# Layer parameters loaded and turned ahead of the modulation's products, rotary tables behind the normed rows, in a two-layer trunk

## The chip, the core and the metric

The kernel runs on one core of a Trainium2 chip. The metric is device time in microseconds (us), the median of several executions. The engines are named as in the profile: PE is the matrix engine (PEld its weight loads), DVE, ACT and POOL are the three elementwise engines, SP issues most of the DMAs, and a trailing q ("SPq", "ACTq", "POOLq") marks an engine's instruction queue, where DMAs are issued.

## What is computed

A trunk of two layers over 1024 rows of width 1024, cut here to what matters at the start:

```
c_act = silu(c)
for l in range(2):
    mod = c_act @ ada_w[l] + ada_b[l]                  # 1024 x 6144
    sh1, sc1, gt1, sh2, sc2, gt2 = split(mod, 6)
    h = rms_norm(x, norm1_g[l]) * (1.0 + sc1) + sh1
    proj = h @ w_in[l]                                 # q, k, v and the RWKV inputs
    q, k = partial_rotary(q, cos, sin), partial_rotary(k, cos, sin)
    mixed = concat(diff_attention(q, k, v), rwkv7_time_mix(proj[..., 1536:])) @ w_out[l]
    x = x + gt1 * mixed
    h2 = rms_norm(x, norm2_g[l]) * (1.0 + sc2) + sh2
    x = x + gt2 * hier_moe(h2)                         # 32 experts, two for each row
return rms_norm(x, final_g)
```

`cos` and `sin` come from the positions alone.

## The kernel before

Each engine works through its own instruction list in order. The kernel is traced in Python, and then a scheduler with a model of the engines' times lays out the order of each list; `issue_after(x)` adds no wait of its own but forbids the scheduler to put the instructions of its block ahead of `x` in the list of `x`'s engine. So both the text of the program and the model decide what stands ahead of what.

The start of layer 0 goes like this. `before()` in `build` makes constants, loads the first four of the eight tiles of x (128 rows each), and runs `modulation(0, range(4), ...)`: blocks 0 to 3, which give the shift `sh1` and the scale `sc1`. A block is four loads of `ada_w` (512 KB each, called chunks below), 32 narrow products into `ada_ps` (L238, eight for each chunk), an addition of the bias on DVE into `modE` (L241), a turn of `modE` on PE into `ada_t` (L244), and a copy into the table `mv` on DVE (L245). Then, behind the last `ada_w` load, `params(0, ...)` fetches 14 small rows through POOL's queue into `prow`, turns them on PE (`prow_ps`, L276) and copies them into `pv` on DVE (L279); `first_weights` fetches and splits the first two slices of `w_in` (`wa_raw` into `wa_hi` and `wa_lo`, L348 and L349); and the last four tiles of x are loaded.

`norm1` takes the squares of a tile on ACT (L317, into `n_j`), the inverse root for two tiles at a time (L100 on DVE, L102 on ACT, L107 to L109 on DVE, ending in `rs_y_n`), scales the rows (`n_y`, L325), turns them on PE (`n_t`, L332), and applies scale `g1` (L328, from `mv` and `pv`) and shift on ACT (`n_tmp`, L334). DVE and ACT split the result into `hh` and `hl` (L337, L338), and PE multiplies both with `wa_hi` and `wa_lo` into `pj` (L361 to L363). `prow_ps` and `n_t` share two PSUM banks. The eight 128-column pieces of a half of the rows are gone through one by one, and the second half follows.

From there on `phase_a` weaves projections, the RWKV scan (tiles `rb_*`, with the state `b_sb`) and attention (`at_*`). Between them PE does what `more` yields: the modulation's blocks 4 to 11 of layer 0 and all 12 of layer 1 in chunks with two buffers, and after the first eight chunks `tables`, which makes the rotary tables (`rotary_tables`, L159 to L199) and loads layer 1's parameters. Then come the output projection and the mixture of experts, and layer 1 does the same again.

Of the kernel before, what the change touches and what calls it, by code (L numbers as in the profile page):

```python
# [10 lines left out]
F32 = mybir.dt.float32  # L11
# [4 lines left out]
OP = mybir.AluOpType  # L16
# [36 lines left out]
class Trunk:  # L53
# [243 lines left out]
    def norm1(self, l, tile_of, work, psum):  # L297

        nc = self.nc
        self.hh = [self.big.tile([128, T], F32R, name=f"hh{k}", tag=f"hh{k}") for k in range(NK)]  # L300
        self.hl = [self.big.tile([128, T], F32R, name=f"hl{k}", tag=f"hl{k}") for k in range(NK)]
        g1 = work.tile([128, 8], F32, name="g1")
        xs, order = [], ExitStack()
        for g in range(2):
            if g and l:

                for x in (root, xs[-1][1]):
                    order.enter_context(self.tc.issue_after(x.ins))
            if g:
                xs = []  # L310
            for i in range(4):
                if i % 2 == 0:
                    ss = work.tile([128, 2], F32, name="n1_ss", tag="n1_ss", bufs=2)
                    pair = []
                x = tile_of(4 * g + i)
                junk = work.tile([128, D], F32, name="n1_j", tag="n1_j", bufs=1)
                nc.scalar.activation(junk, x, AF.Square, accum_out=ss[:, i % 2:i % 2 + 1])  # L317
                pair.append(x)
                if i % 2:
                    rs = self.rsqrt(work, ss, 2, NORM_EPS, 1.0 / D, "n1", act=True)  # L320
                    root = self.last_root
                    for q, x in enumerate(pair):
                        y = work.tile([128, D], F32, name="n1_y", tag="n1_y", bufs=4)
                        xs.append((y, nc.scalar.activation(y, x, AF.Copy, scale=rs[:, q:q + 1]) if l else
                                   nc.vector.tensor_scalar(y, x, rs[:, q:q + 1], None, op0=OP.mult)))  # L325
            order.close()
            if g == 0:
                nc.vector.scalar_tensor_tensor(g1, self.mv[l][:, 8:16], 1.0, self.pv[l][0][:, 0:8], op0=OP.add, op1=OP.mult)  # L328
            for k in range(NK):
                pt = psum.tile([128, 4, 128], F32, name="n1_t", tag="aa")  # L330
                for i in range(4):
                    nc.tensor.transpose(pt[:, i, :], xs[i][0][:, k * 128:(k + 1) * 128], self.ident)  # L332
                tmp = work.tile([128, 512], F32, name="n1_tmp", tag="n1_tmp", bufs=2)
                nc.scalar.activation(tmp, pt.rearrange("p a b -> p (a b)"), AF.Identity,  # L334
                                     bias=self.mv[l][:, k:k + 1], scale=g1[:, k:k + 1])
                hi, lo = self.hh[k][:, 512 * g:512 * g + 512], self.hl[k][:, 512 * g:512 * g + 512]
                (nc.scalar.copy if k % 2 else nc.vector.tensor_copy)(hi, tmp)  # L337
                nc.vector.tensor_tensor(lo, tmp, hi.bitcast(F32), op=OP.subtract)  # L338


    def split_w(self, wp, l, i, eng=None):
# [79 lines left out]
    def phase_a(self, l, x_src, psum, here, there):  # L421

        nc, a, tc = self.nc, self.a, self.tc
# [10 lines left out]
        more = iter(())  # L434
        if l == 0:
            wpool = sm.enter_context(self.pool(name="adaw", bufs=2, side=there))
            work = sm.enter_context(self.pool(name="adax", bufs=1, side=there))
            rows = self.modulation(0, range(4, 12), wpool, work, psum, 2)
            more = itertools.chain(itertools.islice(rows, 8), self.tables(work, psum), rows,
                                   *(self.modulation(j, range(12), wpool, work, psum, 2) for j in range(1, L)))  # L440

        def wtile(c0):
# [171 lines left out]
        if True:  # L614
            self.when["R", 0] = 0.0
            self.agents = []
            for rank, g in ((0, self.rwkv_second(l, late, sf, there, psum)), (4, firsts()), (6, projects()), (7, tables()), (8, tail()),
                            (9, heads())):
                self.add(rank, g)
            self.weave()  # L620
# [1202 lines left out]
    def final(self, pool):  # L1823
# [4 lines left out]
        for t in range(0, NT, 2):  # L1828
# [7 lines left out]
            for i in range(2):  # L1836
                nc.vector.scalar_tensor_tensor(os[i], self.xm[:, t + i, :], rs[:, i:i + 1], fg, op0=OP.mult, op1=OP.mult)  # L1837
                nc.scalar.dma_start(self.out[0, 128 * (t + i):128 * (t + i) + 128, :], os[i])  # L1838

    def tables(self, work, psum):  # L1840

        self.clear_tinv(work)
        yield
        self.rotary_tables(work)
        yield
        for l in range(1, L):
            self.params(l, work, psum)
            yield
# [73 lines left out]
    def build(self):  # L1922
        ctx, nc = self.ctx, self.nc
        self.cst = ctx.enter_context(self.pool(name="cst", bufs=1))
        self.lay = ctx.enter_context(self.pool(name="lay", bufs=1))
        self.dram = ctx.enter_context(self.pool(name="dram", bufs=1, space=DRAM))
        self.mrow, self.mv, self.pv, xs = {}, {}, {}, []

        def before():
            work = self.norm_pool  # L1930
            self.constants()
            self.conditioning(work, self.psum)

            def load(t):
                x = work.tile([128, D], F32, name=f"x{t}")
                nc.sync.dma_start(x, self.a["x"][0, 128 * t:128 * t + 128, :])
                xs.append(x)

            for t in range(4):
                load(t)  # L1940
            with ExitStack() as s:
                wpool = s.enter_context(self.pool(name="ada0", bufs=13))
                for _ in self.modulation(0, range(4), wpool, work, self.psum, 2):
                    pass
            with self.tc.issue_after(self.ada_load.ins):
                self.params(0, work, self.psum)
                self.first_weights(0)
                for t in range(4, 8):
                    load(t)

        self.start(0, "left", lambda t: xs[t], before)
        x_src = lambda t: self.a["x"][0, 128 * t:128 * t + 128, :]
        for l in range(self.layers):
            x_src = self.layer(l, x_src)
# [48 lines left out]
```

## Time and profile before

| What | Value |
|---|---|
| Median of 3 runs | 2689.37 us (2685.37 to 2702.67) |
| The profiled execution | 2696.09 us, span of its instructions 2694.1 us |
| PE busy | 2389.1 us, 89% of the span |
| DVE busy | 1852.7 us, 69% |
| ACT busy | 1193.2 us, 44% |
| POOL busy | 313.7 us, 12% |
| Mean granted clock of PE | 0.918 |

The profile is one execution. Its shares are averages over stages with different limits: the change touches the first 100 us, where PE is idle for a good part, so the stretch's own rows count there and not the 89%. A granted clock of 1.00 in a row is 2.4 GHz, 0.50 is 1.2 GHz, and values between are means over a stretch that has both.

### The profile page before, as it was taken

The page shows a single profiled execution, that of the slowest core. Times are in us where ns is not written, and L with a number is a line of the kernel's source. Part 1 is how long each engine was busy: PE and PEld are TensorE (multiplying, and loading weights), DVE is VectorE, ACT ScalarE, POOL GpSimd, SP SyncE. Part 2 cuts the span into 40 slices and gives each one's busy share as a digit, 9 for nine tenths or more (in the row PEclk, how much of TensorE's full clock was granted, in tenths as well). Part 3 has the DMA queues.
Part 4 walks back from the last instruction along what each step waited for, and adds up shares of the span by engine and source line. Part 5 has one row for each costly group of instructions (what it writes and reads, how often), then busy time and mean ns, then how long its engine had stood idle before and what let it go on. Part 6 is the DMA issues. An engine that isn't in the chain of part 4 may idle for free. (4 is left out here: it accounts for less than half of the span.)

```text
span 2694.1 us, 45448 instructions
## 1 busy us (share of the span) xinstructions
PE 2389.1 (89%) x17313; PEld 1826.6 (68%) x17313; DVE 1852.7 (69%) x4053; ACT 1193.2 (44%) x2316; POOL 313.7 (12%) x251
## 2 busy tenths in 40 slices
PE   6999998898889979999959989989997996999992
PEld 3666666777767866777736767767776885677771
DVE  4347767656579486877764588965658847787775
ACT  3344443234256224555545555424426622555552
POOL 3100000000000002333310000000000001333330
PEclk8998998789989979999979989899988997999996
DMA  8566765525354247999942434445336325899985
GB/s 295 175 214 205 211 210 166 155 91 148 93 171 126 95 171 290 354 338 359 369 174 103 147 113 143 141 140 166 117 89 193 104 97 195 319 385 348 336 307 202
DMA packets 263940, 542.68 MB, mean 201 GB/s; under 512 B 76504, under 2 KB 180896, under 8 KB 234784
## 3 DMA queue, kind: packets, MB, share of 16 engines
q1 hardware_dynamic: 235712, 484.61, 53.9%
q0 software_dynamic: 23376, 40.99, 4.1%
q10 hardware_dynamic: 4624, 14.06, 1.4%
q8 instruction: 141, 2.31, 0.4%
q14 instruction: 87, 0.71, 0.1%
HBM read 459.29 MB, written 120.09 MB: 215 GB/s over the span
## 5 line engine op out<-in xcount | busy, mean ns | idle before, releaser
L1646 DVE TENSOR_TENSOR w_lo<-w_gu,w_hi 128x2048 fp32r<-128x2048 f32 x134 | 306.3, 2286 | 69.2 <-ACT w_hi L1645 69.0
L1645 ACT CAST w_hi<-w_gu 128x2048 fp32r<-128x2048 f32 x134 | 255.7, 1908 | 211.2 <-PE h_ps L1698 204.5
L361 PE MATMUL pj<-hh,wa_hi 128*128 128x512 f32 x800 | 335.2, 419 | 2.1 <-ACT wa_hi L348 1.7
L362 PE MATMUL pj<-hl,wa_hi 128*128 128x512 f32 x800 | 332.2, 415 | 1.1 <-DVE hl L338 1.0
L363 PE MATMUL pj<-hh,wa_lo 128*128 128x512 f32 x800 | 325.5, 408 | 0.1
L1737 PE MATMUL y_ps<-w_d,hT 128*128 128x512 f32 x560 | 252.2, 593 | 3.4 <-ACTq L1798 2.4
L1697 PE MATMUL h_ps<-w_hi,xT_hi 128*128 128x512 f32 x560 | 243.0, 434 | 4.4 <-ACT xT_hi L1681 4.4
L1698 PE MATMUL h_ps<-w_hi,xT_lo 128*128 128x512 f32 x560 | 222.6, 398 | 2.5 <-DVE xT_lo L1682 2.5
L1699 PE MATMUL h_ps<-w_lo,xT_hi 128*128 128x512 f32 x560 | 222.4, 397 | 0.0
L1726 POOL DMA_INDIRECT yd<-yo,idx_s x70 | 183.6, 2623 | 290.2 <-DVE yo L1723 275.4
L361 PEld LDWEIGHTS pj<-hh,wa_hi 128*128 128x128 f32 x800 | 156.2, 195 | 41.5 <-issue 6.0
L362 PEld LDWEIGHTS pj<-hl,wa_hi 128*128 128x128 f32 x800 | 155.8, 195 | 37.0 <-issue 4.0
L363 PEld LDWEIGHTS pj<-hh,wa_lo 128*128 128x128 f32 x800 | 155.2, 194 | 35.4 <-issue 3.6
L1737 PEld LDWEIGHTS y_ps<-w_d,hT 128*128 128x128 f32 x560 | 100.9, 190 | 104.8 <-issue 100.4
L1697 PEld LDWEIGHTS h_ps<-w_hi,xT_hi 128*128 128x128 f32 x560 | 107.3, 192 | 38.0 <-issue 11.5
L1698 PEld LDWEIGHTS h_ps<-w_hi,xT_lo 128*128 128x128 f32 x560 | 107.3, 192 | 36.7 <-DVE th L1689 11.5
L1682 DVE TENSOR_TENSOR xT_lo<-xT_ps,xT_hi 128x1024 fp32r<-128x1024 f32 x70 | 85.7, 1225 | 65.8 <-ACT xT_hi L1681 65.8
L1699 PEld LDWEIGHTS h_ps<-w_lo,xT_hi 128*128 128x128 f32 x560 | 107.0, 191 | 23.0
L1723 DVE SCALAR_TENSOR_TENSOR yo<-y_ps,wsl,gt 128x1024 f32<-128x1024 f32 x70 | 89.8, 1283 | 38.3 <-PE y_ps L1737 38.3
L1192 ACT ACTIVATE at_p<-at_s,at_mx 128x256 f32<-128x256 f32 (+7 forms) x128 | 94.8, 741 | 40.6 <-DVE at_mx L1190 39.8
L1190 DVE TENSOR_REDUCE at_mx<-at_s 128x1 f32<-128x256 f32 (+7 forms) x128 | 95.6, 752 | 14.5 <-PE at_s L1188 13.3
L238 PE MATMUL ada_ps<-ada_w,crep 128*32 128x128 f32 x1536 | 71.9, 313 | 37.6 <-DMA ada_w<-in_ada_w 37.4
(436 smaller groups left out, 4949.3 us busy)
## 6 DMA issues: line engine op xcount, KB each, us to landing
w_gu<-in_moe_w_gu SPq DMA_DIRECT2D x140, 1024.0 KB
w_d<-in_moe_w_down SPq DMA_DIRECT2D x70, 1024.0 KB
ada_w<-in_ada_w SPq DMA_DIRECT2D x96, 512.0 KB
wa_raw<-in_w_in SPq DMA_DIRECT2D x50, 512.0 KB
sp_z<-z SPq DMA_DIRECT2D x32, 768.0 KB
b_zz<-sp_z SPq DMA_DIRECT2D x32, 512.0 KB
cy<-yd SPq DMA_DIRECT2D x16, 1024.0 KB
qkv<-qst SPq DMA_DIRECT2D x48, 256.0 KB
```

What stands on the lines that cost most here:

```text
L361: nc.tensor.matmul(ps, hi[:, k, :], self.hh[k][:, sl], start=(k == 0), stop=False)
L362: nc.tensor.matmul(ps, hi[:, k, :], self.hl[k][:, sl], start=False, stop=False)
L363: nc.tensor.matmul(ps, lo[:, k, :], self.hh[k][:, sl], start=False, stop=(k == NK - 1))
L1190: nc.vector.tensor_reduce(mx, ps[:, 0:n], axis=AX.X, op=OP.max, negate=True)
L1192: nc.scalar.activation(pm[:, 0:n], ps[:, 0:n], AF.Exp, bias=mx, accum_out=hs["s"][:, t, m:m + 1])
L1645: self.nc.scalar.copy(hi, raw)
L1646: eng.tensor_tensor(lo, raw, hi.bitcast(F32), op=OP.subtract)
L1697: nc.tensor.matmul(ph, hi[:, k, :], whi[:, k % 4, :], start=(k == 0), stop=False)
L1698: nc.tensor.matmul(ph, lo[:, k, :], whi[:, k % 4, :], start=False, stop=False)
L1699: nc.tensor.matmul(ph, hi[:, k, :], wlo[:, k % 4, :], start=False, stop=(k == NK - 1))
L1726: st = nc.gpsimd.indirect_dma_start(out=self.yd, out_offset=bass.IndirectOffsetOnAxis(ap=self.idx_s[:, e:e + 1], axis=0), in_=yos[e % 2], ...
L1737: nc.tensor.matmul(po[:, 512 * half:512 * half + 512], hT[:, k, :], w[:, k, 512 * half:512 * half + 512], start=(k == 0), stop=(k == 1))
```

## The change

`params(0, ...)` is called ahead of the modulation's blocks 0 to 3, outside the block that stands behind the last `ada_w` load. And each step of `tables` is traced inside `issue_after(self.last_lo)`: no instruction of the rotary tables and of layer 1's parameters may stand ahead of the last `hl` of `norm1` in DVE's list.

```
@@ norm1
-                nc.vector.tensor_tensor(lo, tmp, hi.bitcast(F32), op=OP.subtract)
+                self.last_lo = nc.vector.tensor_tensor(lo, tmp, hi.bitcast(F32), op=OP.subtract)
@@ phase_a
-            more = itertools.chain(itertools.islice(rows, 8), self.tables(work, psum), rows,
+            more = itertools.chain(itertools.islice(rows, 8), self.behind(self.last_lo, self.tables(work, psum)), rows,
@@ new
+    def behind(self, x, g):
+
+        while True:
+            with self.tc.issue_after(x.ins):
+                try:
+                    next(g)
+                except StopIteration:
+                    return
+            yield
@@ build, before()
+            self.params(0, work, self.psum)
             with ExitStack() as s:
                 wpool = s.enter_context(self.pool(name="ada0", bufs=13))
                 for _ in self.modulation(0, range(4), wpool, work, self.psum, 2):
                     pass
             with self.tc.issue_after(self.ada_load.ins):
-                self.params(0, work, self.psum)
                 self.first_weights(0)
```

The scheduler lays the lists out anew. Three places follow. In DVE's list, after the scaled rows of the first four tiles of x, there stood before (`modE` is a block's sum with its bias, `mv` its copy, `rs_*_500` the inverse root for x's fifth and sixth tiles):

```order
L325 TENSOR_SCALAR n_y<-x_131,rs_y_n_411 128x1024
L241 TENSOR_TENSOR modE<-ada_ps,ada_bias 128x128
L245 COPY mv_122<-ada_t 128x4
L241 TENSOR_TENSOR modE<-ada_ps,ada_bias 128x128
L245 COPY mv_122<-ada_t 128x4
L241 TENSOR_TENSOR modE<-ada_ps,ada_bias 128x128
L245 COPY mv_122<-ada_t 128x4
L241 TENSOR_TENSOR modE<-ada_ps,ada_bias 128x128
L165 MEMSET freq 128x1
L348 CAST wa_hi<-wa_raw 128x1024
```

and now, in the same list from the split of the first slice of `w_in` on (the five operations of `params` stand between `n_y` and this):

```order
L348 CAST wa_hi<-wa_raw 128x1024
L349 TENSOR_TENSOR wa_lo<-wa_raw,wa_hi 128x1024
L100 TENSOR_SCALAR rs_v_n_500<-n_ss 128x2
L107 SCALAR_TENSOR_TENSOR rs_u_n_502<-rs_v_n_500,rs_y_n_501 128x2
L108 TENSOR_TENSOR rs_u_n_502<-rs_u_n_502,rs_y_n_501 128x2
L109 SCALAR_TENSOR_TENSOR rs_y_n_501<-rs_u_n_502,rs_y_n_501 128x2
L241 TENSOR_TENSOR modE<-ada_ps,ada_bias 128x128
L100 TENSOR_SCALAR rs_v_n_517<-n_ss 128x2
L245 COPY mv_122<-ada_t 128x4
```

The first `modE`, block 0's, has moved behind the split of the first slice and behind the root of the fifth and sixth tiles; the other three blocks' follow later still.

In PE's list, from its first instructions on, before:

```order
L207 MATMUL c_ps<-ident,crow 128x8
L238 MATMUL ada_ps<-ada_w,crep 32x128 x32
L244 MATMUL ada_t<-ident,modE 128x128
L238 MATMUL ada_ps<-ada_w,crep 32x128 x32
L244 MATMUL ada_t<-ident,modE 128x128
L238 MATMUL ada_ps<-ada_w,crep 32x128 x32
L244 MATMUL ada_t<-ident,modE 128x128
L238 MATMUL ada_ps<-ada_w,crep 32x128 x32
L244 MATMUL ada_t<-ident,modE 128x128
L276 MATMUL prow_ps<-ident,prow 128x42
L332 MATMUL n_t<-ident,n_y 128x128 x8
L238 MATMUL ada_ps<-ada_w,crep 32x128 x8
```

and now:

```order
L238 MATMUL ada_ps<-ada_w,crep 32x128 x32
L276 MATMUL prow_ps<-ident,prow 128x42
L332 MATMUL n_t<-ident,n_y 128x128 x8
L244 MATMUL ada_t<-ident,modE 128x128
L238 MATMUL ada_ps<-ada_w,crep 32x128 x32
L244 MATMUL ada_t<-ident,modE 128x128
L238 MATMUL ada_ps<-ada_w,crep 32x128 x32
L244 MATMUL ada_t<-ident,modE 128x128
L238 MATMUL ada_ps<-ada_w,crep 32x128 x32
L244 MATMUL ada_t<-ident,modE 128x128
L238 MATMUL ada_ps<-ada_w,crep 32x128 x8
L332 MATMUL n_t<-ident,n_y 128x128 x4
```

The turn of the parameters and the first eight turns of normed rows have moved ahead of block 0's turn; the products of blocks 1 to 3 still stand behind that turn, and block 4's first chunk directly behind block 3's turn.

In SP's list of DMAs, after the last tile of x, before:

```order
L235 DMA ada_w<-in_ada_w 128x1024 x2
L160 DMA pos_i<-in_positions 128x8x1
L345 DMA wa_raw<-in_w_in 128x1024
L877 DMA b_lnx<-in_rwkv_lnx_g 128x128
L877 DMA b_lnx<-in_rwkv_lnx_b 128x128
L235 DMA ada_w<-in_ada_w 128x1024 x2
L345 DMA wa_raw<-in_w_in 128x1024
```

and now:

```order
L345 DMA wa_raw<-in_w_in 128x1024 x2
L235 DMA ada_w<-in_ada_w 128x1024 x2
L160 DMA pos_i<-in_positions 128x8x1
L877 DMA b_lnx<-in_rwkv_lnx_g 128x128
L877 DMA b_lnx<-in_rwkv_lnx_b 128x128
L235 DMA ada_w<-in_ada_w 128x1024 x10
```

The second and third slice of `w_in` have moved ahead of block 4's first two chunks. Those chunks still take memory that block 3's last products free.

## Rows read from the trace of the kernel before

**Rows 1.** The page: busy time, share of the span and instructions of each engine.

```profile
PE 2389.1 (89%) x17313; PEld 1826.6 (68%) x17313; DVE 1852.7 (69%) x4053; ACT 1193.2 (44%) x2316; POOL 313.7 (12%) x251
```

**Rows 2.** Stretches: length, busy time by engine, granted PE clock, DMA share, GB/s.

```profile
28.00:30.00 2.00, 1.08 (x16) 0.59 (x16) 0.00 (x0) 0.00 (x0) 1.65 (x4) 0.50 1.03 390
...
44.50:50.00 5.50, 5.46 (x44) 3.99 (x45) 4.87 (x17) 4.18 (x7) 0.00 (x0) 0.50 0.58 174
...
50.00:55.00 5.00, 5.00 (x53) 3.59 (x51) 4.24 (x11) 3.15 (x5) 0.00 (x0) 0.98 0.79 216
...
80.00:90.00 10.00, 10.00 (x76) 5.13 (x65) 3.21 (x6) 4.65 (x6) 0.00 (x0) 1.00 0.35 116
```

**Rows 3.** One stretch, from the first to the tenth chunk of blocks 4 to 6.

```profile
44.54:72.55 28.01, 25.19 (x239) 17.65 (x239) 20.70 (x55) 17.51 (x27) 0.00 (x0) 0.90 0.64 198
```

**Rows 4.** PE in order of time: start, length, what, count, idle before and releaser.

```profile
19.18 3.02 PE L238 MATMUL ada_ps<-ada_w,crep 128*32 128x128 f32 x48
...
31.91 4.19 PE L238 MATMUL ada_ps<-ada_w,crep 128*32 128x128 f32 x64
...
41.88 1.12 PE L332 MATMUL n_t<-ident,n_y 128*128 128x128 f32 x4 [3.54 <-DVE pv L279]
44.54 1.08 PE L238 MATMUL ada_ps<-ada_w,crep 128*32 128x128 f32 x16 [1.55 <-DMA ada_w<-in_ada_w]
```

**Rows 5.** DVE in order of time.

```profile
31.16 0.29 DVE L241 TENSOR_TENSOR modE<-ada_ps,ada_bias 128x128 f32<-128x128 f32 x1 [6.96 <-PE ada_ps L238]
...
36.17 0.29 DVE L241 TENSOR_TENSOR modE<-ada_ps,ada_bias 128x128 f32<-128x128 f32 x1 [3.99 <-PE ada_ps L238]
...
37.11 0.16 DVE L245 COPY mv<-ada_t 128x4 f32<-128x4 f32 x1
...
41.55 0.16 DVE L109 SCALAR_TENSOR_TENSOR rs_y_n<-rs_u_n,rs_y_n 128x2 f32<-128x2 f32 x1
41.62 0.20 DVE L279 COPY pv<-prow_ps 128x42 f32<-128x42 f32 x1
...
42.15 0.16 DVE L328 SCALAR_TENSOR_TENSOR g<-mv,pv 128x8 f32<-128x8 f32 x1
```

**Rows 6.** ACT in order of time: squares of the sixth and eighth tile, first scaled piece.

```profile
39.53 1.06 ACT L317 ACTIVATE n_j<-x 128x1024 f32<-128x1024 f32 x1 [0.80 <-DMA x<-in_x]
...
43.31 1.06 ACT L317 ACTIVATE n_j<-x 128x1024 f32<-128x1024 f32 x1 [0.99 <-DMA x<-in_x]
...
44.36 0.76 ACT L334 ACTIVATE n_tmp<-n_t,mv,g 128x512 f32<-128x512 f32 x1
```

**Rows 7.** SP's DMA issues in order of time.

```profile
25.85 5.56 SPq L1936 DMA_DIRECT2D x<-in_x  x4
36.17 1.57 SPq L235 DMA_DIRECT2D ada_w<-in_ada_w  x2
...
53.34 20.98 SPq L235 DMA_DIRECT2D ada_w<-in_ada_w  x8
```

**Rows 8.** PE's chunks of blocks 4 to 6, in order of time.

```profile
47.88 1.08 PE L238 MATMUL ada_ps<-ada_w,crep 128*32 128x128 f32 x16
...
58.15 0.64 PE L238 MATMUL ada_ps<-ada_w,crep 128*32 128x128 f32 x16 [0.52 <-DMA ada_w<-in_ada_w]
60.56 0.64 PE L238 MATMUL ada_ps<-ada_w,crep 128*32 128x128 f32 x16 [0.48 <-DMA ada_w<-in_ada_w]
...
72.55 0.64 PE L238 MATMUL ada_ps<-ada_w,crep 128*32 128x128 f32 x14
```

**Rows 9.** DVE's groups of 47 to 66 us by shape; the table's first use.

```profile
L185 DVE TENSOR_TENSOR ang_r<-ang_r,ang_m 128x64 f32<-128x64 f32 x2 | 0.4, 221 | 0.0
...
L1054 DVE TENSOR_TENSOR xc<-qst,cos x32: 273/282/289, 341.7 to 2006.6; 128x128 f32<-128x128 f32 x32
```

**Rows 10.** What PE waited for, 300 to 850 us; a stretch in it.

```profile
PE rb_s L896 <- DVE b_sb L898: 15.7, 11, 4.2
...
450.00:500.00 50.00, 39.78 (x411) 31.97 (x406) 41.11 (x120) 13.03 (x30) 0.00 (x0) 0.67 0.53 132
```

## The prediction, made before the changed kernel ran

> **What bounds the kernel now.** Read the page first: PE is busy for 89% of the span [rows 1], so a delay of PE early on has little room to be made up for later. The change touches the first 100 us, so next come the stretches there, the waits of PE, and then each engine in order of time. Up to about 44 us the start lives on loads: the DMA share is 1.03 with PE at work for 1.08 of 2.00 us [rows 2], and the last four tiles of x, issued from 25.85 on [rows 7], reach ACT as late as 39.53 (sixth) and 43.31 (eighth) [rows 6]. In this time PE computes blocks 0 to 3 as their chunks come: block 1 starts at 19.18, block 3 runs from 31.91 and ends at 36.1 [rows 4], and the last copy into `mv` ends at 37.3 [rows 5]. Two things then stand in a row behind x's sixth tile: DVE's list has the root of tiles five and six (ends 41.71) ahead of `pv` (41.62) and `g1` (42.15) [rows 5], and PE, which needs the PSUM bank of `prow_ps`, stands for 3.54 us [rows 4]. The first `n_tmp` starts at 44.36, on the heels of the eighth tile's square [rows 6]. From 44.5 to about 75 us PE, ACT, DVE and the chunks of blocks 4 to 6 keep each other waiting; from 80 us PE is the bound, 10.00 of 10.00 us [rows 2].
>
> **The change, part 1: the parameters early.** The 14 loads and the turn of `prow` now end long before they are needed, and the 3.54 us wait for `pv` goes. That alone buys almost nothing: behind that wait the next thing late is ACT, whose list still holds the squares of all four late tiles ahead of the first `n_tmp`, and that one followed the eighth square directly [rows 6]. `ada_bias` is now queued on POOL behind these 14 loads. Its first reader is block 0's `modE`, which will be late for another reason, so I cost this at nothing; without that cover it would be some microseconds.
>
> **Part 2: what the new order does to DVE and PE.** This is where I see the price. Block 0's `modE` now stands in DVE's list behind the split of the first `w_in` slice and behind the root of x's fifth and sixth tiles. In the trace that root ends at 41.71 [rows 5]. PE's list has block 0's turn, which needs this `modE`, ahead of the products of blocks 1 to 3. So PE, which now begins block 1 at 19.18, will stand from about 20 us until about 41, with all 12 chunks lying ready (13 buffers).
>
> Step by step. The sixth tile may land a little earlier, because two chunks (1 MB) issued at 36.17 [rows 7] are no longer in its way, while a `w_in` slice of half that size is instead. I bound the root's end by 39.7 (two microseconds for the whole MB) and 41.7 (no change) and take the middle, 40.7. From a `modE` to the next block's first product the trace has 31.16 to 31.91, or 0.75 us [rows 4, 5]: block 1 starts at 41.45. A block's products take 4.19 us at the low clock [rows 4] and 4 x 0.64 = 2.56 us at the full one [rows 8]; between blocks lie 0.85 us (the 0.75, and a tenth for the end of the products before). All three at the low clock end at 41.45 + 3 x 4.2 + 2 x 0.85 = 55.75; with only the first at it, at 52.5. PE will come out of 20 idle microseconds; in the trace it was at 0.50 (1.2 GHz) in sparse work from 28 us on, worked densely from 44.5, and was at 0.98 in the stretch from 50 [rows 2], so after some 5.5 us. The same span here gives the full clock at about 47, early in block 2, and an end at **52.8**. In the trace that end was 36.1.
>
> From the last `modE` to the end of its `mv` copy it is 1.1 us [rows 5], and `g1` takes 0.2 more: the first `n_tmp` starts at 54.3, where it started at 44.36. So the roots of the last tiles are no longer the bound, and `pv` never was.
>
> **Part 3: the first chunk of block 4.** PE's list has it right behind block 3's turn, and its load takes memory that block 3's last products free: in the trace it was issued at 36.17 [rows 7], 0.07 after those ended, and its products waited till 44.54 [rows 4]. Now the issue comes at 52.9. With the queue less full, an issue took 4.8 us to its products (53.34 to 58.15, the wait for the DMA shown) [rows 7, 8]; the nearest lower bound is 2.4 us, at which chunks follow each other (58.15, 60.56) [rows 8]. I take 4.8, since this one is a whole load behind its issue: 57.7, against 44.54, so **+13.2 us**. Behind it on PE stand the next turns of rows, and all of `norm1` behind those.
>
> The Trainium skill ("DMA: Bandwidth & Descriptors", its table of the two cost components) gives about 2.0 us fixed and the bytes at 436 GB/s, 3.2 us for 512 KB by an estimate from it. The 4.8 us measured here are longer, with other loads in flight; by the page the step would be 1.6 us smaller.
>
> **Part 4: what the norm stage gives back.** From the first chunk of block 4 to the tenth it took 44.54 to 72.55, 28.0 us [rows 3]. In it 5.5 us went by at the low clock [rows 2], and DVE worked out the rotary tables: 20 operations of some 0.22 us [rows 9], 4.4 us. Both go out of the stage. What remains are two buffers: a chunk that is freed comes back after 4.8 us, and its products take 0.64 [rows 8], so two chunks for 5.44 us. The second chunk's products started 3.3 us behind the first's (47.88) [rows 8]; four rounds more make 25.1 us. So -2.9 us. The ends are 0 (the turns and `n_tmp` set the pace as before) and -5.5 (all of the 2.8 us in which PE idles there, 28.01 less 25.19 [rows 3], and half of 5.46 us at the low clock [rows 2]).
>
> **Part 5: the tables late.** These operations and eight small fills now stand behind the last `hl`, at 85 to 105 us, where DVE is busy 3.21 of 10 us [rows 2], and the tables' first reader comes at 341.7 [rows 9]. PE hides them: nothing. If they pushed a `pj` bank's emptying they would cost PE at most their 4.4 us once. Layer 1's parameters go with them and have even more room.
>
> **Part 6: the rest.** PE's list is the same from about 76 to 440 us, and PE-bound, so the delay is carried on. Behind that the lists of both layers' scan and attention stretches are reordered in places, with the same work: of the 32 scan steps one has another number of projections ahead of it, and six another number of attention products, by 3 to 7. I take zero, with some 10 us either way.
>
> **Sum.** +13.2 - 2.9 = +10.3 us. The profiled execution took 2696.1 (its span 2694.1), 6.7 over the median; it would become 2706.4, and the median 2689.4 + 10.3 = **2699.7**. By the bounds: early tile, short load and full give-back, 10.3 - 1 - 2.4 - 2.6 = +4.3; late tile, low clock throughout, no give-back, 10.3 + 1 + 3 + 2.9 = +17.2. The likeliest case's own range is 2693 to 2707.
>
> **Rivals.**
> 1. *Not slower: the reordered scan stretches fill PE's waits.* Between 300 and 850 us PE waits 11 times, 15.7 us, for the scan's state `b_sb` on DVE [rows 10]. The new order moves attention products past some scan steps exactly there. Filling all of it gives 2699.7 - 15.7 = 2684. It decides from two thirds of these waits on. Against it: the scan steps have kept their places against the projections. 0.12.
> 2. *Slower by over 1%: the clock.* In 450 to 500 us the granted clock is 0.67 with PE busy 39.78 us [rows 10]; if a reordered wait sends another such stretch to 0.50, its 40 us cost 20 more: 2720. It decides from about 17 us on. 0.07.
> 3. *The change does what its words say.* If block 0's `modE` is not held up, `pv` is early, the tables' 4.4 us leave DVE in a stretch where it is busy 4.87 of 5.5 us [rows 2], and up to 4 us come of it: 2685.5. It needs the root of the sixth tile done before about 19 us, and that tile is issued after 25.85 [rows 7], or a DVE that takes its list out of order. 0.03.
>
> **How the numbers follow.** The forecast has 0.75; another 0.03 is for what I don't see. 1% of the time before, 27 us, is about what a measurement here can tell from no change. The forecast and rivals 1 and 3 lie within it; over 27 us slower come from rival 2 and the far end of part 6: 0.08. Faster by that much would take more than every wait of rival 1: 0.02. Within: 0.90. The range covers rival 1's 2684 and stops short of rival 2: 2683 to 2717.
>
> **What would show it.** Right: PE idle from about 20 to 41 us behind L244 with DVE's `modE` as releaser; the first `modE` at about 40.7; blocks 1 to 3 in one run, the first of them at 1.08 us a chunk; the first `n_tmp` at 54; block 4's first chunk near 57.7 after a wait for its DMA, and the tenth about 25 us on; no wait for `pv`. PE's rows of 100 us should come 10 us later, and the start of the experts in layer 0 too. Wrong: a first `modE` near 18 (rival 3), or a delay at 100 us that is gone by 850 (rival 1).

## The result, and the profile after

The changed kernel took **2710.27 us** (median of 16 runs) beside 2693.44 us of the kernel before (16 runs on the same chip): a ratio of **1.0055, 95% interval 1.0039 to 1.0070**, some 15 us slower and well within 1%. A second timing (experiment 8) gave 1.0049 (1.0030 to 1.0068). One execution each of experiments 4 and 11, at 8233 and 5558 us, is left out of the ratios below. The profiled execution took 2716.71 us, 6.4 above its own median, and its mean granted clock, 0.913, is the lowest of the 16 (their median is 0.9215), so its later offsets are read with care.

The page: PE is busy for 3 us more than before, in a span that is 20.8 longer, so most of what was lost is standing [rows 1].

```profile
PE 2392.3 (88%) x17313; PEld 1832.6 (68%) x17313; DVE 1857.8 (68%) x4053; ACT 1193.7 (44%) x2316; POOL 314.8 (12%) x251
```

PE in order of time answers to [rows 4]. Block 0's turn (L244) starts after 21.40 us of standing for DVE's `modE`; then blocks 1 to 3 go through in one run, 64 products a row; then the first chunk of block 4 stands for its load.

```profile
39.58 0.48 PE L244 MATMUL ada_t<-ident,modE 128*128 128x128 f32 x1 [21.40 <-DVE modE L241]
39.98 3.45 PE L238 MATMUL ada_ps<-ada_w,crep 128*32 128x128 f32 x64
...
44.12 1.95 PE L238 MATMUL ada_ps<-ada_w,crep 128*32 128x128 f32 x64
...
46.74 1.95 PE L238 MATMUL ada_ps<-ada_w,crep 128*32 128x128 f32 x64
...
53.83 1.08 PE L238 MATMUL ada_ps<-ada_w,crep 128*32 128x128 f32 x16 [4.39 <-DMA ada_w<-in_ada_w]
```

DVE in order of time, against [rows 5]: `pv` is done at 17 us; then DVE stands for the load of the first `w_in` slice, splits it, works out the root of x's fifth and sixth tiles, and only then comes block 0's `modE`, whose products had lain ready since 17 us. (Its bias came later than that: experiment 4, where these loads are queued alike, waits for it until 19.9.)

```profile
17.20 0.20 DVE L279 COPY pv<-prow_ps 128x42 f32<-128x42 f32 x1 [1.26 <-PE prow_ps L276]
...
34.55 0.69 DVE L348 CAST wa_hi<-wa_raw 128x1024 fp32r<-128x1024 f32 x1 [16.72 <-DMA wa_raw<-in_w_in]
...
39.05 0.16 DVE L109 SCALAR_TENSOR_TENSOR rs_y_n<-rs_u_n,rs_y_n 128x2 f32<-128x2 f32 x1
39.23 0.29 DVE L241 TENSOR_TENSOR modE<-ada_ps,ada_bias 128x128 f32<-128x128 f32 x1
...
49.67 0.17 DVE L328 SCALAR_TENSOR_TENSOR g<-mv,pv 128x8 f32<-128x8 f32 x1
```

Before, the same `modE` waited for its products alone:

```profile
18.43 0.29 DVE L241 TENSOR_TENSOR modE<-ada_ps,ada_bias 128x128 f32<-128x128 f32 x1 [2.62 <-PE ada_ps L238]
```

ACT, against [rows 6]: the squares of the sixth and the eighth tile come 2.5 and 3.6 us earlier than before, and the first scaled piece, for which ACT now stands 8.59 us until `g`, 5.5 us later.

```profile
37.04 1.06 ACT L317 ACTIVATE n_j<-x 128x1024 f32<-128x1024 f32 x1
...
39.70 1.06 ACT L317 ACTIVATE n_j<-x 128x1024 f32<-128x1024 f32 x1
...
49.87 1.45 ACT L334 ACTIVATE n_tmp<-n_t,mv,g 128x512 f32<-128x512 f32 x2 [8.59 <-DVE g L328]
```

SP's issues, against [rows 7]: the `w_in` slices now go ahead of block 4's chunks, which are issued at 48.76 in place of 36.17.

```profile
25.61 4.17 SPq L1946 DMA_DIRECT2D x<-in_x  x4
36.53 7.17 SPq L345 DMA_DIRECT2D wa_raw<-in_w_in  x2
48.76 0.81 SPq L235 DMA_DIRECT2D ada_w<-in_ada_w  x2
```

Stretches, against [rows 2, 3] (length, PE, PE's loads, DVE, ACT, POOL, granted clock, DMA share, GB/s). PE works 0.42 of the 20 us from 20 to 40 and is at the full clock from 44 to 50; when block 4's first chunk comes, it is at the lower one again for a while (0.92 over 50 to 54, 0.77 over 54 to 60). The last row goes from the first to the tenth chunk of blocks 4 to 6: 26.69 us, where it was 28.01.

```profile
20.00:40.00 20.00, 0.42 (x4) 0.20 (x4) 2.86 (x7) 3.84 (x8) 0.00 (x0) 0.57 1.00 397
40.00:44.00 4.00, 3.58 (x66) 3.07 (x65) 2.62 (x8) 1.05 (x3) 2.61 (x5) 0.61 0.13 41
44.00:50.00 6.00, 4.61 (x131) 3.65 (x130) 1.23 (x6) 0.13 (x1) 5.66 (x12) 1.00 0.48 130
50.00:54.00 4.00, 0.17 (x4) 0.20 (x8) 2.22 (x3) 1.94 (x3) 2.73 (x6) 0.92 0.88 297
54.00:60.00 6.00, 6.00 (x56) 4.63 (x52) 1.81 (x3) 2.71 (x4) 0.00 (x0) 0.77 0.60 130
...
53.83:80.52 26.69, 24.65 (x240) 17.55 (x240) 14.85 (x26) 14.01 (x20) 0.00 (x0) 0.95 0.59 171
```

Following the same products through both traces, the offset is +9.3 us at block 4's first chunk (53.83 against 44.54), +8.0 at the tenth and at the first product of L460 (86.54 against 78.55), +10.6 at 255 us of the time before, +13.7 at 1475, and +20.5 from 2260 to the end. So some 8 us come from the front that the prediction was about, and this execution lost more behind it. The experiments ask how much of that belongs to the change. The first product of L460, before:

```profile
78.55 1.04 PE L460 MATMUL pj<-hh,wa 128*32 128x512 f32 x8
```

and now:

```profile
86.54 1.04 PE L460 MATMUL pj<-hh,wa 128*32 128x512 f32 x8
```

### The profile page after: what moved, and what is told of

It is laid out like the page before. It is cut to its first block, busy times and chain, and to the rows that moved or that the text cites. A ratio compares the mean times of both kernels' runs of the same rounds, so it can differ in the third digit from the quotient of the medians.

```text
span 2714.9 us, 45442 instructions
## 1 busy us (share of the span) xinstructions
PE 2392.3 (88%) x17313; PEld 1832.6 (68%) x17313; DVE 1857.8 (68%) x4053; ACT 1193.7 (44%) x2316; POOL 314.8 (12%) x251
## 5 line engine op out<-in xcount | busy, mean ns | idle before, releaser
L1698 PEld LDWEIGHTS h_ps<-w_hi,xT_lo 128*128 128x128 f32 x560 | 107.3, 192 | 36.8 <-DVE th L1689 11.2
L751 DVE TENSOR_TENSOR sv_m<-sv_t,sv_n 64x31 f32<-64x31 f32 (+15 forms) x248 | 82.0, 330 | 33.1 <-DMA sv_n<-sp_z 26.9
```

Of the source, the lines that this page charges most:

```text
L1698: nc.tensor.matmul(ph, lo[:, k, :], whi[:, k % 4, :], start=False, stop=False)
```

## The experiments

The scheduler lays out all later lists anew with every edit, so a part of the change cannot be run alone without other differences. Most kernels below therefore hold the lists of all engines behind the front (from some 85 us on, both layers) to those of another kernel: the names of its instructions, engine by engine, are written into the kernel as `ORDER`, and neighbours are tied by edges that set the order and make nobody wait. This adds some lines, so line numbers shift.

```diff
+        traced = {i.name: i for b in at for i in b.bb.instructions}
+        for row in listed(ORDER):
+            for x, y in zip(row, row[1:]):
+                self.tc.add_manual_dep(traced[f"I-{y}"], f"I-{x}", mybir.DependencyInfo(mybir.DependencyClass.NoSync, mybir.DependencyReason.DATA),
+                                       reason="listed order")
```

All twelve were timed in five rounds beside the kernel before, whose medians were 2696.84 (1 to 4), 2694.36 (5 to 8) and 2695.18 us (9 to 12). Each experiment has 12 executions (7, 8 and 6 in experiments 7, 8 and 9). Microseconds are the ratio less one, times that median. "Front" is the first product of L460, at 78.55 before.

| Experiment | Front, us against before | Ratio (95% interval) | us |
|---|---|---|---|
| 1 front of the change, lists of before | +9.5 | 1.0038 (1.0022 to 1.0055) | +10.2 |
| 2 front of before, lists of the change | +0.1 | 1.0004 (0.9990 to 1.0018) | +1.1 |
| 3 the change, layer 1's lists of before | +8.3 | 1.0039 (1.0026 to 1.0052) | +10.5 |
| 4 the change with `modE` first, lists of before | -3.0 | 1.0014 (0.9998 to 1.0029) | +3.8 |
| 5 parameters early alone, lists of before | +11.2 | 1.0042 (1.0026 to 1.0058) | +11.3 |
| 6 tables late alone, lists of before | +2.0 | 0.9998 (0.9981 to 1.0015) | -0.5 |
| 7 block 0's `modE` late alone, lists of before | +10.2 | 1.0048 (1.0030 to 1.0065) | +12.9 |
| 8 the change again | +7.2 | 1.0049 (1.0030 to 1.0068) | +13.2 |
| 9 that `modE` later still, lists of before | +24.7 | 1.0107 (1.0074 to 1.0140) | +28.8 |
| 10 as 4, squares late | +4.7 | 1.0018 (0.9995 to 1.0041) | +4.9 |
| 11 as 10, products first | 0.0 | 1.0006 (0.9983 to 1.0029) | +1.6 |
| 12 as 4, lists free | -4.0 | 1.0018 (0.9998 to 1.0037) | +4.9 |

### Is it the front or the lists? (1, 2, 3)

The theory at this point, T: the front costs some 8 us, the reordered lists the rest. Rivals: the front is everything (F), or the lists are (L).

Experiment 1 is the changed kernel with `ORDER` from the kernel before.

> The change, but with the lists of every engine behind the first 85 us (both layers) held to the order that they have before the change; only the front differs from before. Theory T (the front carries some 8 us to the end, the rest of the +15 us comes from the reordered lists): +7 to +10 us against before, first L460 at 86.5, and the same offset of 8 us at 500, 1000 and 2000 us. Rival F (the front is the whole loss, and grows on its way): +13 to +17. Rival L (the front is made up for later, the lists are the loss): 0 to +3.

Experiment 2 is the kernel before with `ORDER` from the changed one.

> The other half: the kernel before, but with the lists of every engine behind the first 85 us held to the order of the changed kernel. Theory T: +5 to +8 us, none of it before 140 us, some 5 us between 140 and 1000 us and the rest in layer 1's scan stretch. Rival F: within 2 us of before. Rival L: +13 to +17.

Experiment 3 is the changed kernel with `ORDER` from before, of layer 1 alone.

> The change with layer 1's lists alone held to the order before. Against the changed kernel it tells what layer 1's reordering costs. Theory T: +11 to +13 us against before, the offset of 13 us at the end of layer 0 stays to the end. Rival F: as the change, +13 to +17, with an offset that still grows in layer 1. Chance (the growth in layer 1 is that of one profiled execution): the same median as the change.

Measured: +10.2, +1.1 and +10.5 us. L falls with the first two. The front is most of the loss; T's 5 to 8 us for the lists were too much, since the upper end of experiment 2 is +4.9. F's 13 to 17 us for experiment 1 lies above its middle, though its interval reaches 14.8. Front and lists by themselves make 11.3 us, the two timings of the change 14.8 and 13.2; with intervals of 4 to 5 us to each side that is no contradiction. Experiment 8, the change timed beside experiments 5 to 7, was to give +9 to +13 if the two parts add up and +14 to +18 if they multiply each other; its +13.2 (8.1 to 18.3) does not decide between these.

A small price of layer 1's lists can be seen in the traces. PE's waits there, between some 1465 and 2205 us (us in total, times, longest): before, with the old lists:

```profile
PE at_s L1185 <- ACT at_p L1192: 18.0, 12, 8.7
PE qk_t L1030 <- ACT qst L1072: 5.7, 4, 4.7
...
PE rb_s L896 <- DVE b_sb L898: 3.3, 6, 1.2
```

The changed kernel, with the new ones:

```profile
PE at_s L1185 <- ACT at_p L1192: 16.0, 11, 7.9
PE rb_s L896 <- DVE b_sb L898: 14.7, 8, 5.1
```

Experiment 1, the change's front with the old lists again:

```profile
PE at_s L1188 <- ACT at_p L1195: 17.4, 11, 8.1
PE qk_t L1033 <- ACT qst L1075: 6.0, 4, 4.9
...
PE rb_s L899 <- DVE b_sb L901: 3.6, 6, 1.2
```

With the new lists PE waits 11 us more for the scan's state, and saves the waits for `qst` and some for `at_p`. From the start of layer 1's first product into `nb` to that of its last into `po` the new lists took 775.2, 775.5 and 775.1 us (the change, experiments 8 and 2), the old ones 770.1, 771.8, 773.9 and 773.1 (before, 1, 3 and 4) and 767.7 to 771.9 in the six other traces that have them: 1 to 8 us more with the new ones. Layer 0's new lists showed no sign of their own: between 255 and 1475 us of the time before, the offset grew by 3.1, 7.2 and 3.1 us in the change and experiments 8 and 3, and fell by 8.1 in experiment 2; with the old ones it moved by anything from -6.5 (experiment 10) to +10.6 (experiment 5).

### Which part makes the front? (5, 6, 7)

Experiment 5 leaves the tables where they were:

```diff
-            more = itertools.chain(itertools.islice(rows, 8), self.behind(self.last_lo, self.tables(work, psum)), rows,
+            more = itertools.chain(itertools.islice(rows, 8), self.tables(work, psum), rows,
```

> Only the parameters early; the rotary tables stay in the norm stage, and the later lists are held to the order before. Block 0's modE stands in DVE's list where the change has it. Theory (the place of this modE is the price, the tables' 20 operations on DVE are worth what the norm stage gives back): front as in the first experiment, so +9 to +13 us against before. If the late tables were what costs: 0 to +3.

Experiment 6 undoes the other part:

```diff
-            self.params(0, work, self.psum)
             with ExitStack() as s:
 ...
             with self.tc.issue_after(self.ada_load.ins):
+                self.params(0, work, self.psum)
                 self.first_weights(0)
```

> Only the tables behind the last hl, the parameters at their old place, the later lists held to the order before. modE comes as before (first one near 17.5 us), PE still waits some 3.5 us for pv. Theory: first L460 0 to 3 us earlier, -3 to +1 us at the end. If the late tables cost: +5 or more, with a wait for sin or cos, or a later emptying of pj, between 85 and 110 us.

Experiment 7 does neither. It is the kernel before with one edge of order on DVE:

```diff
+            if l == b == 0:
+                self.first_mode = add
...
                     root = self.last_root
+                    if l == 0 and g == 1 and i == 1:
+                        self.tc.add_manual_dep(self.first_mode.ins, root.ins.name, mybir.DependencyInfo(mybir.DependencyClass.NoSync, mybir.DependencyReason.DATA),
+                                               reason="behind the root")
```

> The kernel before, parameters and tables at their old places, with one edge of order added: block 0's modE stands behind the root of x's fifth and sixth tiles in DVE's list (blocks 1 to 3 follow it, and with them the place of the turn of prow in PE's list). Later lists held to the order before. Theory (this one place is the whole price): first modE at 39 to 41.5 us, first L460 8 to 12 us later, and +8 to +13 us at the end. If the early parameters themselves (their 14 loads, the turn, the first turns of rows) make the price: 0 to +3.

Measured: +11.3, -0.5 and +12.9 us. The late tables neither cost nor bring anything that can be measured, though the first L460 came 2.0 us later in experiment 6, not earlier as expected; by 255 us its offset was -1.1. PE in it still waits for `pv`, as in [rows 4]:

```profile
41.57 1.12 PE L335 MATMUL n_t<-ident,n_y 128*128 128x128 f32 x4 [3.58 <-DVE pv L282]
```

Experiment 7 has the parameters at their old place, and the whole loss. The chain is that of the changed kernel: root, `modE`, turn, and the chunk that waits for its load. DVE in order of time:

```profile
38.54 0.16 DVE L112 SCALAR_TENSOR_TENSOR rs_y_n<-rs_u_n,rs_y_n 128x2 f32<-128x2 f32 x1
38.75 0.29 DVE L244 TENSOR_TENSOR modE<-ada_ps,ada_bias 128x128 f32<-128x128 f32 x1
```

PE in the same execution:

```profile
39.09 0.47 PE L249 MATMUL ada_t<-ident,modE 128*128 128x128 f32 x1 [20.61 <-DVE modE L244]
...
53.48 0.64 PE L241 MATMUL ada_ps<-ada_w,crep 128*32 128x128 f32 x16 [3.82 <-DMA ada_w<-in_ada_w]
```

So the place of one 0.29 us operation in DVE's list is enough for the price. What the edge drags along is part of it, as in the changed kernel: the `w_in` slices go ahead of block 4's chunks on SP there too. In the changed kernel's trace these slices are not what block 4's first chunk waits for: from 47 to 49 us, when that chunk is issued (48.76), the DMAs move 9 GB/s, so the queue before it is empty.

### Is a delay of the front carried to the end? (9)

Experiment 9 is the seventh with a larger dose:

```diff
                     if l == 0 and g == 1 and i == 1:
+                        row = [root]
+                        for _ in range(9):
+                            d = work.tile([128, 1], F32, name="pause", tag="pause", bufs=1)
+                            row.append(nc.vector.tensor_reduce(d, x, op=OP.max, axis=AX.X))
+                        row.append(self.first_mode)
+                        for x, y in zip(row, row[1:]):
+                            self.tc.add_manual_dep(y.ins, x.ins.name, ...)
```

> The seventh experiment with a larger dose: nine reductions of a 128x1024 tile to one column, whose results nobody reads, stand on DVE between the root and block 0's modE, some 10 us. With D the further delay of this modE against the 38.75 us of the seventh experiment, the theory (the front's delay is carried to the end as it is) says: first L460 D later than there, and the end D later too, so about +23 us against before for D = 10. If the norm stage or later waits swallow part of a delay: less than +18. If a longer standing of PE costs more than its length: over +28.

DVE in order of time, with the last four of the nine reductions:

```profile
46.59 4.98 DVE L331 TENSOR_REDUCE pause<-x 128x1 f32<-128x1024 f32 x4
51.49 0.28 DVE L244 TENSOR_TENSOR modE<-ada_ps,ada_bias 128x128 f32<-128x128 f32 x1
```

PE, the first chunk of block 4:

```profile
66.23 1.08 PE L241 MATMUL ada_ps<-ada_w,crep 128*32 128x128 f32 x16 [4.22 <-DMA ada_w<-in_ada_w]
```

`modE` came 12.74 us later than in experiment 7, block 4's first chunk 12.75, the first L460 14.5 (103.20 against 88.71), and the end 15.9 us later (28.8 less 12.9, each with some 5 to 9 us of uncertainty; the medians of the two, each less its own before's, differ by 9.4). With D the expectation is 12.9 + 12.7 = +25.6; the ratio gives 20 to 38 and the medians 23.3. The bounds set for D = 10, 18 and 28, become 20.7 and 30.7 for this D, and 28.8 lies between them. That is D carried on as it is, within what the timing tells.

### Can it be mended, or turned into a gain? (4, 10, 11, 12)

Experiment 4 keeps the split and the roots of the late tiles behind the last copy into `mv`, on DVE alone:

```diff
-                nc.vector.tensor_copy(self.mv[l][:, 4 * b:4 * b + 4], pt[:, 0:128:32])
+                self.last_mv = nc.vector.tensor_copy(self.mv[l][:, 4 * b:4 * b + 4], pt[:, 0:128:32])
...
-            if g and l:
-                for x in (root, xs[-1][1]):
+            if g:
+                for x in (root, xs[-1][1]) if l else (self.last_mv,):
                     order.enter_context(self.tc.issue_after(x.ins))
...
-                self.first_weights(0)
+                with self.tc.issue_after(self.last_mv.ins):
+                    self.first_weights(0)
```

> The change (parameters early, tables late) with the split of the first w_in slices and the roots of x's last four tiles kept behind the last copy into mv in DVE's list, and the later lists held to the order before. Theory T (the price of the front is block 0's modE behind that split and that root): block 0's modE at about 18 us, no 20 us of standing on PE, the first n_tmp at 39 to 44, block 4's first chunk at 41 to 45, and -4 to +1 us against before. If something else of the early parameters is the price (ada_bias behind 14 loads on POOL, the earlier w_in slice on SP), the chunk stays at 50 or later and the run at +6 or more.

The edges bring `modE` back to 19.90 us (DVE's row below), and here the cover is gone under which `ada_bias` was costed at nothing: the operation now waits for that load, and starts 1.5 us later than the 18.43 of before.

```profile
19.90 0.29 DVE L244 TENSOR_TENSOR modE<-ada_ps,ada_bias 128x128 f32<-128x128 f32 x1 [1.41 <-DMA ada_bias<-in_ada_b]
```

On PE the stand of 20 us is gone, `pv` is early, and yet the first chunk of block 4 comes only 1.6 us earlier than before: its load, issued at 36.15 among those of x, is what PE now waits for. A second wait for a chunk stands at 178 us, as before (there 3.66 us, up to 179.88).

```profile
42.91 1.08 PE L241 MATMUL ada_ps<-ada_w,crep 128*32 128x128 f32 x16 [5.94 <-DMA ada_w<-in_ada_w]
...
178.20 1.08 PE L241 MATMUL ada_ps<-ada_w,crep 128*32 128x128 f32 x16 [3.79 <-DMA ada_w<-in_ada_w]
```

So most of the price goes (from +10.2 to +3.8 with the same later lists; the medians of the two, timed side by side, differ by 10.0 us), and what the words of the change promise is worth 2 to 3 us at the front. At the end nothing of that is left: +3.8 us, above the -4 to +1 that theory T expected, with no change inside the interval. By its trace the offset was -2.2 at 189 us, +0.3 at 255 and +1.3 at the end; why it is not below zero at the end I can't say from these runs.

Experiment 10 also keeps the squares of x's last four tiles behind the fourth `n_tmp`, by adding that instruction to the tuple `(self.last_mv,)` above.

> The fourth experiment, and the squares of x's last four tiles kept behind the fourth n_tmp in ACT's list, so that nothing of x's late tiles stands ahead of the first half's norm. First n_tmp at some 38 us in place of 43.0. If the first half's norm bounds the stage: first L460 3 to 5 us earlier than before, -5 to 0 us at the end. If block 4's first chunk does (its load landed at 42.9): no earlier than in the fourth experiment, -1 to +4 us.

Experiment 11 adds an edge by which block 4's first product stands behind the projection's sixth.

```diff
+            if k == 1 and self.block4 is not None:
+                self.tc.add_manual_dep(self.block4.ins, x.ins.name, ...)
```

> The tenth experiment, and block 4's first chunk moved behind the first six products of the projection in PE's list, so that PE doesn't stand for this load from 37 to 43 us. If PE's standing there is worth its length: first products L363 kind at some 40 us, first L460 4 to 7 us earlier than before, -7 to -2 us at the end. If the two chunk buffers set the pace of the stage up to 75 us: L460 within 2 us of the tenth experiment's.

Experiment 12 is the fourth without `ORDER`.

> The fourth experiment as it would be used, with the later lists left to the scheduler, which lays out layer 0 anew and layer 1 otherwise than before. If the lists behind the front are worth no more than a few microseconds whichever they are: within 4 us of the fourth experiment's +3.8. If the layout matters: anything over 8 us away from it.

Measured: +4.9, +1.6 and +4.9 us, none of them apart from before. In experiment 10 the first `n_tmp` on ACT indeed starts at 38.69, 5.7 us earlier than before:

```profile
38.69 1.45 ACT L336 ACTIVATE n_tmp<-n_t,mv,g 128x512 f32<-128x512 f32 x2 [24.95 <-DVE g L330]
```

But PE's first chunk of block 4 comes at 44.81, and its first L460 4.7 us later than before, behind a wait of 1.99 us for a `w_in` slice:

```profile
44.81 1.08 PE L241 MATMUL ada_ps<-ada_w,crep 128*32 128x128 f32 x16 [7.04 <-DMA ada_w<-in_ada_w]
...
83.20 1.93 PE L464 MATMUL pj<-hh,wa 128*32 128x512 f32 x8 [1.99 <-DMA wa<-in_w_in]
```

In experiment 11 PE starts its first projection product at 40.31, in the time in which it stood for that load in experiment 10, and yet the first L460 comes at 78.52, 0.03 us from the kernel before. An earlier beginning of the norm's first half is worth nothing by itself; neither guess of what bounds that stage is shown, beyond that it isn't this. Experiment 12 ends 1.1 us from the fourth by ratio, so the layout behind the front again made no difference that can be told. Its profiled execution was 10.9 us ahead of before's at the end while its median was slower: one trace's late offset is worth some 10 us, no better. Part of this goes with the clock: that execution's mean granted clock, 0.928, is the highest of its 12, and of the 90 executions of the kernel before that were timed beside the experiments, the 15 at 0.919 or less have a median of 2700.9 us, the 21 at 0.925 or more one of 2689.8. No version here beats the kernel before.

## Why the prediction was right

It said 2699.7 us, +10.3, within 1%, by a front that is late; the two timings say +14.8 and +13.2, and the front alone +10.2 (experiment 1). The prediction took 27 us for about the least that a measurement here tells from no change; the two timings have 4 to 5 us to each side.

- **The mechanism.** That block 0's `modE` is held behind the `w_in` split and the root of x's sixth tile, that PE stands from 20 to 40 us, and that block 4's chunk is late behind it: right in each step, and shown by experiments 7 (that place alone: +12.9) and 4 (that place undone: +3.8). That the delay is carried on unchanged: experiments 7 and 9, within their intervals.
- **Part 1, the parameters early.** The 3.54 us wait for `pv` is gone and bought nothing that lasts, as said: experiment 4 has the early `pv` without the hold-up and is not faster. The 14 loads were not late before either: POOL issued them from 3.90 to 14.63 us, and from 1.43 to 11.15 in the changed kernel. What moved is their turn on PE (36.99 to 16.90) and `pv` on DVE (41.62 to 17.20), which stood late in the lists. `ada_bias` behind 14 loads costs 1.4 us of wait once its cover is gone.
- **Part 2, sizes.** `modE` came at 39.23, where 40.7 was put, and below the range for the root (it ended at 39.21, the range began at 39.7): the sixth tile's square came 2.5 us earlier, not 1, and for the most part not for the reason that I gave (last section). Blocks 1 to 3 ended at 48.7, not 52.8. Two terms were too large: the clock was up again before the second block (3.45 us for the first, 1.95 for the others), where I had carried over the 5.5 us that it took before (and had misread them, as the last section shows); and a block at the full clock is 1.95 us as one row of 64, not four times the 0.64 of a separate row of 16.
- **Part 3.** From issue to products 5.07 us, where 4.8 was put. By the Trainium skill ("DMA: Bandwidth & Descriptors", the two cost components) an estimate was 3.2; its fit there is for loads that GpSimd issues. The trace disagrees again, and decides: this load was issued by SP, with a second chunk right behind it. The step as a whole was +9.3, not +13.2, all of the difference from part 2.
- **Part 4, the give-back.** -1.3 us to the tenth chunk, where -2.9 was put and 0 to -5.5 allowed. The second chunk came 3.86 us behind the first, not 3.3, and the four rounds after it took 5.71 us each, not 5.44. The low clock, which I had going out of this stage, stayed in part: from 53.83 to 56.40 us it was granted 0.50 with PE busy throughout, and the first chunk took 1.08 us. The first L460 came 8.0 us late in place of 10.3.
- **Part 5, the tables.** Nothing, as said (experiment 6).
- **Part 6, the rest.** Put at zero with 10 us either way. Experiment 2 gives +1.1 (-2.7 to +4.9); the traces give layer 1's new lists a price of 1 to 8 us, with 11 us more of waiting for `b_sb` beside it. So the sum came out near because errors offset each other, which is luck in the size, not in the mechanism: the step to block 4's chunk 3.9 us too large, the give-back 1.6 too large, the rest some microseconds too small. The remainder between +11 and +14 lies within the intervals and is not explained.
- **Rivals.** The filled scan waits (1) did not come: in the stretch that this rival named, 300 to 850 us, PE waited 17.3 us for `b_sb`, against 15.7 [rows 10], and in layer 1 these waits grew. The clock (2) did not: the median granted clock of the 16 executions is 0.9215, that of the 90 of the kernel before 0.922, and 450 to 500 us had 0.80 in the profiled execution, against 0.67. Its price was too large as well: 39.78 us at 0.67 become 53.3 at 0.50, 13.5 more and not 20. That the change does what its words say (3) is not seen to pay either: experiments 4, 10, 11 and 12 come nearest to that case, at +1.6 to +4.9, and of their intervals only that of experiment 11 reaches down to -4. PE's waits in the changed kernel, 300 to 850 us:

```profile
PE rb_s L896 <- DVE b_sb L898: 17.3, 13, 5.2
```

## What to carry to other kernels

When a piece of setup is moved to an earlier place, ask of every in-order list what now stands ahead of the operations that were there: here a 0.29 us addition, whose products were ready at 17 us and whose bias at some 20, was laid behind operations that needed loads which landed between 34 and 37, and TensorE stood 21 us for it. In this kernel, bound by one engine for most of its time, a delay at the head was paid in full at the end, within the intervals (experiments 7 and 9). Taking one wait out of the head brought little where the next late thing (here the load of the next chunk) came hardly earlier, and a front that was 3 to 4 us early (experiments 4 and 12) did not show at the end, for a reason that stays open. To time one part of such a change, hold the rest of the lists fixed, and trust the medians, not the late offsets of one trace.

## What the runs showed of the hardware

- TensorE's clock rose sooner than I had carried over, and fell again. Before, it was granted 0.50 (1.2 GHz) throughout 44.5 to 50 us with PE busy for 5.46 of 5.50 us [rows 2]. The prediction counted dense work from there on alone, but PE was busy at 0.50 for most of 31.51 to 38.33 us too, and the clock did not rise on that:

```profile
31.51:38.33 6.82, 6.31 (x71) 3.78 (x71) 2.32 (x13) 0.74 (x1) 2.47 (x6) 0.50 1.03 404
```

  In the changed kernel, after 21 us of standing, it was 0.50 over 39.58 to 43.05 us with PE busy throughout, 1.00 (2.4 GHz) from 44 to 50, and 0.50 over 53.83 to 56.40, after 4.39 us of standing. By the blocks' own times it differs from run to run: the first three blocks after the standing took 3.45, 1.95 and 1.95 us here, 3.64, 1.95 and 1.95 in experiment 7, and 3.64, 2.35 and 1.95 in experiment 1.
- Products in one run are cheaper than rows of them add up to: 64 took 1.95 us, a separate row of 16 took 0.64 [rows 8]. The end of a row holds some 0.2 us that the next products of the same kind would cover: (1.95 - 0.64) / 48 makes 0.027 us for one, 0.44 for 16. The profile models the ends of matmuls, so a part of that is its reckoning; by the starts, other work followed such a row after 0.58 us (58.15 to 58.73, before).
- While small loads on POOL's queue were under way, the large ones on SP's moved less, by more than the small ones' bytes. The late tiles of x came early for the most part not because two chunks were out of their way: the fifth tile's square started at 35.82 in place of 37.59, before those chunks' issue at 36.17. But the loads of `ada_bias` for blocks 4 to 7 are released by products on PE, and in both traces they start 1.41 us behind the first of block 1's products (19.18 and 39.98). So the late `modE`, which holds these products, also held these loads, and the small ones of layer 1's `prow` behind them, back to 41 to 51 us. On POOL, before:

```profile
20.59 2.24 POOL L229 DMA_DIRECT2D ada_bias<-in_ada_b  x4 [5.96 <-PE ada_ps L238]
```

  and now:

```profile
41.39 2.43 POOL L229 DMA_DIRECT2D ada_bias<-in_ada_b  x4 [26.76 <-PE ada_ps L238]
```

  The transfers of 24 to 31 us, before:

```profile
DMA packets 886, 2.46 MB, mean 351 GB/s; under 512 B 269, under 2 KB 289, under 8 KB 886
...
q1 hardware_dynamic: 600, 2.18, 90.0%
q0 software_dynamic: 286, 0.27, 13.2%
```

  The same 7 us in the changed kernel:

```profile
DMA packets 788, 2.88 MB, mean 411 GB/s; under 512 B 86, under 2 KB 86, under 8 KB 788
...
q1 hardware_dynamic: 788, 2.88, 102.8%
```

  The large loads moved 0.70 MB more without the 0.27 MB of small ones; at 411 GB/s that is 1.7 us, and the fifth tile came 1.8 us earlier. Experiments 4 and 6, in which POOL's loads run in this time, moved 324 and 329 GB/s from 25 to 30 us, and that square started at 37.99 and 37.69; experiments 1 and 7, in which they are held, 410 and 408 GB/s, and 35.73 and 35.31. Where these loads are held, PE stands as well; but from 20 to 25 us before, with PE busy for 3.94 of 5.00 us, the DMAs moved 401 GB/s, so PE's work alone is not it.
